# A decoder step's index stage: turns of keys and values one group later in buffers of their own, weight halves behind page requests, head sums in another bank

## The chip, the cores and the metric

The kernel runs on one core of a Trainium2 chip. The metric is the device time of one execution in microseconds. The core has TensorE (PE, matrix products), VectorE (DVE), ScalarE (ACT), GpSimd (POOL), SyncE (SP, which issues most transfers) and sixteen DMA engines.

## The reference

One layer of a hybrid decoder step: a prompt of 1024 tokens and eight decoding sequences of four new tokens each, with 8192 cached positions in pages of 128. An input projection feeds sparse attention (a lightweight indexer picks the 256 best keys) and retention; both are gated and merged. The change is in the part that scores the sequences' cached keys, beside which the prompt's queries, keys, values and gates are projected:

```python
def _project(h, w_in, pos):
    z = jnp.einsum('btd,de->bte', h, w_in)
    ...
    qa, ka, va, qi, ki, wi, ga, qb, kb, vb, gb = jnp.split(z, offsets, axis=-1)
    ...

def _index_select(qi, wi, ki, qpos, kpos, topk):
    s = jnp.einsum('bqhd,bsd->bqhs', qi.astype(jnp.float32), ki.astype(jnp.float32)) * (D_IDX ** -0.5)
    score = jnp.einsum('bqh,bqhs->bqs', wi.astype(jnp.float32), jax.nn.relu(s))
    ...
    top_val, top_idx = lax.top_k(score, topk)

def _dsa_sample(qa, ka, va, qi, ki, wi, cache_k, cache_v, cache_kidx, page_table, rel_bias):
    ...
    ki_past = cache_kidx[page_table].reshape(B, past, D_IDX).astype(ki.dtype)
    ki_all = jnp.concatenate([ki_past, ki], axis=1)
    idx, ok = _index_select(qi, wi, ki_all, qpos, kpos, topk)
    ...

def _merge(x, oa, ob, ga, gb, p, w_out, g_post, w_ple_up, w_ple_gate):
    ya = jax.nn.silu(ga) * oa.reshape(B, T, D_A).astype(x.dtype)
    ...
```

Outputs are the new hidden states, and the keys, values, index keys and retention states of this step.

## The kernel before

The kernel is one program in the Tile framework: the Python code names tiles and instructions, and a scheduler, which simulates a timeline, sets the order of each engine's instructions within what data, buffers and `issue_after` demand. So moving a line can move others. Buffers of one tag rotate: a new tile waits until the readers of the one it replaces are done.

Products are made in pairs of halves: each operand is split into a high part (`whi`, `xh`) and a rest (`wlo`, `xl`), and three products are summed. A projection of 128 columns (`proj_b`) runs over three groups of tokens (`GRP`) of 384, 416 and 256, in this order, with 8 x 3 = 24 matmuls for a group into a bank `pb`. `load_w` brings the weights of 256 columns in two halves `wraw`; for each half ACT makes `whi` by a cast (L202), and POOL subtracts four times for `wlo` (L203). Where `lazy` or `late` is given, `convert` is returned as a generator, and the steps are made by whoever draws on it.

The index stage (L854 to L938) loops over eight sequences `b` and two halves `a` of their pages. In each round POOL requests 1 MB of index keys by an indirect DMA (`key_pages`, L438) into one of two slabs `kx`; DVE transposes them (L913, twice); PE multiplies them with the queries into `pox` (L920); ACT takes the relu `rl` (L925). Then come:

- `later()`: the sum over heads of an earlier sequence (`head_sum`: PE into `py`, L881 and L884, then ACT's copy `ys`, L886), or its re-ordering by key (`by_key`: DVE `xv`, POOL `xe`).
- `step(bp)`: a pass of the bisection that finds the 256th score of the prompt's rows; ACT counts (`js`, L738), DVE counts (L740) and updates the bounds (`W`, `r`, L746 to L771). At its end a flag (`cf`, `pfl`) decides a branch (L805).
- `unit(...)`: one or two projection groups from `units()`: queries `qa`, then keys and values `kava`, then gates `ga0` and `ga1`.

For keys and values ACT copies the projection out of the bank into one half of `kvs` (L466). Ahead of the next group `triple` empties the list `turn`: PE transposes the copy (`kvt`, L475), ACT copies that into the other half of `kvs` (L477), and SP stores it. `kvs` has one buffer. Keys also get a split pair `kst` (ACT L488, DVE L489). For gates, ACT applies Silu to the bank into `sga` (L503), which SP stores. ACT loads the table that holds Silu once in the stage (ACT_TABLE_LOAD at L503).

PE's PSUM banks here: two of tag "b" (`pb`, and `py`), two of tag "t" (`kvt` and other turns), and two pairs of tag "S" (`pox`).

Of the kernel before, what the change touches and what calls it, by code (L numbers as in the profile page):

```python
# [11 lines left out]
F32 = mybir.dt.float32  # L12
# [4 lines left out]
AF = mybir.ActivationFunctionType  # L17
# [19 lines left out]
GRP = ((256, 384), (640, 416), (0, 256))  # L37
# [96 lines left out]
def tile_step(ctx: ExitStack, tc: tile.TileContext, I, O):  # L134
    nc = tc.nc
# [20 lines left out]
    cp = ctx.enter_context(pool("cp"))  # L156
# [3 lines left out]
    def bank(name, tag="b"):  # L160
        if tag in kept.get("tags", ()):
            return kept["pool"].tile([128, 512], F32, tag="s", bufs=1, name=name)
        of = psum["apart" if tag == psum["tag"] else "pool"]
        return of.tile([128, 512], F32, tag=tag, bufs=psum["bufs"][tag], name=name)

    def pair(name):
        return psum["pool"].tile([128, 1024], F32, tag="S", bufs=psum["bufs"]["S"], name=name)
# [3 lines left out]
    def C(name, rows=128):  # L171
        o, w = _CW[name]
        return cst[:rows, o:o + w]

    ident = C("ident")
# [46 lines left out]
    def wcols(*cols):  # L222
        return [(w_in[:, c:c + n], n) for c, n in cols]
# [208 lines left out]
    paged = [None]  # L432

    def key_pages(i):

        b, a = i // 2, i % 2
        kx = slab("kx").bitcast(F32).rearrange("p a b -> p (a b)")
        paged[0] = nc.gpsimd.indirect_dma_start(  # L438
            out=kx[:, :2048], out_offset=None, in_=pages,
            in_offset=bass.IndirectOffsetOnAxis(ap=kidx[:, a * 8 + b:a * 8 + b + 1], axis=0)).ins  # L440
        return kx
# [20 lines left out]

    def use_kv(g, pt, outs, outp, new, then=lambda tk: None):

        st = sx.tile([128, 2, 416], F32, tag="kvs", bufs=1, name="kvs")
        nc.scalar.copy(st[:, 0, :GRP[g][1]], pt[:, :GRP[g][1]])  # L466
        turn.append(lambda: then(turn_kv(g, st, outs, outp, new)))

    def turn_kv(g, st, outs, outp, new):

        t0, n = GRP[g]
        tp = bank("kvt", "t")
        for i in range(0, n, 128):
            rows = min(128, n - i)
            nc.tensor.transpose(tp[:rows, i:i + 128], st[:, 0, i:i + rows], ident)  # L475
        nb = NP[g]
        nc.scalar.copy(st[:, 1, :nb], tp[:, :nb])  # L477
        tk = st[:, 1, :nb].rearrange("p (b c) -> p b c", c=128)
        nc.sync.dma_start(outp[0, 0, t0:t0 + nb].rearrange("(b p) n d -> p b (n d)", p=128), tk)
        if g == SG:  # L480
            nc.vector.tensor_copy(new, tp[:NS, 384:512])
            nc.sync.dma_start(outs.rearrange("o b t n d -> (o b t) (n d)"), new)
        return tk
# [15 lines left out]

    def use_ga(j, g, pt):  # L500
        t0, n = GRP[g]
        sg = qsp.tile([128, 2, 416], F32, tag="qst", bufs=2, name="sga")
        nc.scalar.activation(sg[:, 0, :n], pt[:, :n], AF.Silu)  # L503
        nc.sync.dma_start(ga_d[:, j, t0:t0 + n], sg[:, 0, :n])

    def units():

        def triple(w, c0, use):
            for g in range(3):
                while turn:  # L510
                    turn.pop(0)()
                proj_b(w, c0, 128, use, (g,))
                yield

        w.extend([load_w("qa0", wcols((QA, 256))), load_w("qa1", wcols((QA + 256, 256)))])
        loads = [("kava", KA), ("ga0", GA), ("ga1", GA + 256), None]
        for i in range(5):
            for a in range(2):
                use = ((lambda g, pt: use_qa(2 * i + a, g, pt)) if i < 2 else
                       (use_ka, use_va)[a] if i == 2 else  # L520
                       (lambda g, pt: use_ga(2 * i - 6 + a, g, pt)))
                yield from triple(w[i], a * 128, use)
            if i < 3:
                w.append(load_w(loads[i][0], wcols((loads[i][1], 256)), late=0 if i else 3))

    w = []
    unit_gen = units()
    tick = [0.0]

# [322 lines left out]

    sp_one = cp.tile([128, 1], F32, name="sp_one")
    nc.gpsimd.memset(sp_one, 1.0)  # L854
    bp = bisect_prompt()

    def step(gen, n=1):
        for _ in range(n):
            next(gen, None)
# [5 lines left out]
    for up in range(2):  # L865
        nc.vector.tensor_tensor(wst[:, up], wcol[:, :, None].to_broadcast([128, 8, 32]),
                                C(f"wsel{up}")[:, None, :].to_broadcast([128, 8, 32]), op=ALU.mult)
    pn = bank("pn", "t")
    for h in range(8):
        nc.tensor.matmul(pn[:NS, h * 32:h * 32 + 32], qsn[:, h, :], kis, start=True, stop=True)  # L870
# [5 lines left out]
    nc.vector.tensor_tensor(newsc, newsc, C("nfill", 32), op=ALU.add)  # L876
    pend = []
    def head_sum(b, rls):
        py = bank("py")

        last_ = nc.tensor.matmul(py[96:128, :], wst[:, 1, b, :], rls[3], start=True, stop=True)  # L881
        with tc.issue_after(last_.ins):
            for i in range(3):
                nc.tensor.matmul(py[32 * i:32 * i + 32, :], wst[:, i % 2, b, :], rls[i], start=True, stop=True)  # L884
        ys = sx.tile([128, 512], F32, tag="ys", bufs=2, name="ys")
        nc.scalar.copy(ys, py)  # L886
        nc.sync.dma_start(xt_d[b], ys)
        pend.append(lambda: by_key(b, ys))
# [17 lines left out]
    for b in range(8):  # L906
        rls = []
        for a in range(2):
            kx = key_pages(2 * b + a) if b else kxs[a]
            po = pair("pox")  # L910
            kT = (kx[:, 2048:], kx[:, :1024])
            for up in range(2):
                nc.vector.transpose(kT[up], kx[:, up * 1024:up * 1024 + 1024])  # L913
            head = None
            for up in (1, 0):
                for u2 in range(2):
                    for r in range(2):
                        o, rr = 32 * (2 * (r ^ up) + u2), slice(r * 64, r * 64 + 64)
                        with (tc.issue_after(head) if head else ExitStack()):
                            mm = nc.tensor.matmul(po[o:o + 32, up * 512:up * 512 + 512], qbd[rr, b, :],  # L920
                                                  kT[up][rr, u2 * 512:u2 * 512 + 512], start=True, stop=True,
                                                  tile_position=(64 * r, o))
                        head = head or mm.ins
            rl = sx.tile([128, 1024], F32, tag="rl", bufs=3, name="rl")
            nc.scalar.activation(rl, po, AF.Relu)  # L925
            rls += [rl[:, :512], rl[:, 512:]]
            later()
            tickb[0] += 1.25
            while tickb[0] >= 1:
                tickb[0] -= 1  # L930
                step(bp)
            with tc.issue_after(scored[1]):
                unit((2, 2.5, 2, 2)[2 * b + a] if b < 2 else 12.5 / 12)
        pend.append(lambda b=b, rls=rls: head_sum(b, rls))
# [1167 lines left out]
```

## Time and profile before

| | |
|---|---|
| median of 3 runs | 974.04 us (972.46 to 976.85) |
| profiled execution | 971.68 us, span 969.9 us |
| mean clock granted to PE | 0.984 of full |
| PE busy | 917.9 us, 95% of the span |
| DVE, ACT, POOL busy | 639.4, 458.5, 318.8 us |

The profile is one execution's. A row of its timeline has an instruction's start, its duration, engine, line and tiles; brackets hold the idle time ahead of it and what ended that. A row of stretches gives each engine's busy time, then the clock granted to PE, the share of time that the DMA engines are busy, and GB/s. A row of the chain of waits says which engine and line waited for which, for how long in total, how often, and the longest. Matmuls overlap, so a group's time is read from the starts of its first and of the next group's first.

### The profile page before, as it was taken

How to read it: one execution, taken by the hardware profiler on the slowest of the kernel's cores; microseconds unless marked ns; L12 is line 12 of the kernel's file. 1: busy time of each engine (PE TensorE's matmuls, PEld its weight loads, DVE VectorE, ACT ScalarE, POOL GpSimd, SP SyncE). 2: the span in 40 equal slices, each digit the busy share in tenths (PEclk: the TensorE clock that was granted, in tenths of full speed). 3: DMA queues.
4: the chain of work that ended last, by engine and by line, in shares of the span. 5: the costliest groups of instructions: out<-in, count | busy, mean ns of one | idle time of the engine just before them, and what ended most of it. 6: DMA issues, size and time to landing. Idle time of an engine off the chain costs nothing.

```text
span 969.9 us, 19199 instructions
## 1 busy us (share of the span) xinstructions
PE 917.9 (95%) x7108; PEld 786.8 (81%) x7108; DVE 639.4 (66%) x1898; ACT 458.5 (47%) x1022; POOL 318.8 (33%) x442
## 2 busy tenths in 40 slices
PE   3999999888999999999999988999999999999998
PEld 2988788656779988899889965666668999999998
DVE  6837867878835669978888387877754234943332
ACT  5635654666323886425334284556555334422210
POOL 4205112312415414515344076545204422033300
PEclk8999999988999999999999999999999999999999
DMA  8413224676545110332145445433113222612211
GB/s 261 132 66 83 92 77 153 226 231 197 205 145 124 45 45 24 81 84 63 45 129 164 115 122 167 136 101 103 38 35 87 88 68 77 191 49 94 89 35 39
DMA packets 102129, 104.40 MB, mean 108 GB/s; under 512 B 22002, under 2 KB 92210, under 8 KB 99602
## 3 DMA queue, kind: packets, MB, share of 16 engines
q1 hardware_dynamic: 96274, 76.94, 26.8%
q0 software_dynamic: 5760, 26.22, 8.6%
q8 instruction: 56, 0.92, 0.4%
q14 instruction: 39, 0.32, 0.1%
HBM read 80.38 MB, written 22.76 MB: 106 GB/s over the span
## 4 chain that ended last, share of the span: by engine, by line
PE 54%; DVE 6%; issue 5%; DMA 3%; ACT 2%; POOL 1%; SPq 0%; DVEq 0%; ACTq 0%; POOLq 0%
PE pg L298 3%; PE pg L300 3%; PE pg L299 3%; PE ob L1866 3%; PE ptp L1858 3%; PE po L298 3%; PE po L300 3%; PE po L299 3%; PE pvg L299 2%; PE pvg L298 2%; PE pvg L300 2%; PE sa L1835 2%; PE pqk L298 2%; PE pqk L299 2%; PE pqk L300 2%
## 5 line engine op out<-in xcount | busy, mean ns | idle before, releaser
L1317 POOL DMA_INDIRECT kvs<-in_cache_kv,idx x64 | 67.5, 1054 | 81.8 <-PE pkg L1534 18.5
L298 PE MATMUL pvg<-whi_vgb,xh 128*128 128x256 f32 x256 | 75.2, 294 | 0.5 <-DVE rp L1153 0.5
L299 PE MATMUL pvg<-wlo_vgb,xh 128*128 128x256 f32 x256 | 73.5, 287 | 0.8 <-POOL wlo_vgb L203 0.8
L299 PE MATMUL pqk<-wlo_qkb,xh 128*128 128x256 f32 x256 | 73.9, 289 | 0.0
L298 PE MATMUL pqk<-whi_qkb,xh 128*128 128x256 f32 x256 | 73.8, 288 | 0.1
L300 PE MATMUL pvg<-whi_vgb,xl 128*128 128x256 f32 x256 | 73.7, 288 | 0.0
L300 PE MATMUL po<-whi_o,yTl 128*128 128x256 f32 x256 | 73.1, 285 | 0.4 <-POOL yTl L1914 0.4
L298 PE MATMUL po<-whi_o,yTh 128*128 128x256 f32 x256 | 73.2, 286 | 0.0
L299 PE MATMUL po<-wlo_o,yTh 128*128 128x256 f32 x256 | 72.9, 285 | 0.0
L298 PE MATMUL pg<-whi_g,yTh 128*128 128x256 f32 x256 | 72.8, 285 | 0.0
L300 PE MATMUL pqk<-whi_qkb,xl 128*128 128x256 f32 x256 | 72.8, 284 | 0.0
L300 PE MATMUL pg<-whi_g,yTl 128*128 128x256 f32 x256 | 72.4, 283 | 0.0
L299 PE MATMUL pg<-wlo_g,yTh 128*128 128x256 f32 x256 | 72.3, 283 | 0.0
L1845 ACT ACTIVATE L<-L,mn 128x128 f32<-128x128 f32 (+7 forms) x64 | 49.6, 776 | 22.5 <-DVE mn L1841 22.5
L2057 DVE TENSOR_TENSOR sgm<-pu,sgm 128x256 f32<-128x256 f32 x32 | 13.6, 424 | 64.4 <-PE pu L300 61.1
L203 POOL TENSOR_TENSOR wlo_g<-wraw_g,whi_g 128x256 fp32r<-128x256 f32 x32 | 27.2, 882 | 87.1 <-ACT whi_g L202 87.0
L1858 PEld LDWEIGHTS ptp<-cst,L 128*128 128x128 f32 x288 | 31.6, 142 | 23.8 <-issue 19.4
L298 PEld LDWEIGHTS po<-whi_o,yTh 128*128 128x128 f32 x256 | 49.1, 192 | 2.0 <-issue 1.6
L298 PEld LDWEIGHTS pvg<-whi_vgb,xh 128*128 128x128 f32 x256 | 48.4, 189 | 2.6 <-PE pvg L307 0.8
L298 PEld LDWEIGHTS pg<-whi_g,yTh 128*128 128x128 f32 x256 | 48.8, 191 | 1.6 <-issue 1.2
L569 DVE SCALAR_TENSOR_TENSOR score<-r,wi,score 128x384 f32<-128x384 f32 (+5 forms) x42 | 41.3, 984 | 13.1 <-ACT r L568 10.8
L300 PEld LDWEIGHTS po<-whi_o,yTl 128*128 128x128 f32 x256 | 49.1, 192 | 0.6 <-POOL yTl L1914 0.6
(536 smaller groups left out, 3058.7 us busy)
## 6 DMA issues: line engine op xcount, KB each, us to landing
wraw_qkb<-in_w_in SPq DMA_DIRECT2D x16, 256.0 KB
wraw_vgb<-in_w_in SPq DMA_DIRECT2D x16, 256.0 KB
qas<-qas_d SPq DMA_DIRECT2D x8, 512.0 KB
wraw_o<-in_w_out SPq DMA_DIRECT2D x8, 512.0 KB
xr<-in_x_prompt SPq DMA_DIRECT2D x8, 512.0 KB
wraw_g<-in_w_ple_gate SPq DMA_DIRECT2D x8, 512.0 KB
out_y_prompt<-sgm SPq DMA_DIRECT2D x32, 128.0 KB
qas_d<-qst SPq DMA_DIRECT2D x8, 384.0 KB
```

Source lines behind the costliest of these rows:

```text
L203: nc.gpsimd.tensor_tensor(lo[:, k, :n], raw, hi[:, k, :n].bitcast(F32), op=ALU.subtract)
L298: nc.tensor.matmul(pt[:, :n], ah, hi[:, k, :n], start=(k == 0), stop=False)
L299: nc.tensor.matmul(pt[:, :n], ah, lo[:, k, :n], start=False, stop=False)
L300: nc.tensor.matmul(pt[:, :n], al, hi[:, k, :n], start=False, stop=(k == kc - 1))
L569: nc.vector.scalar_tensor_tensor(sc, r[:, :n], wi[:, qb, h:h + 1], sc if h else place[:, :n], op0=ALU.mult, op1=ALU.add)
L1317: return nc.gpsimd.indirect_dma_start(out=dst, out_offset=None, in_=kvflat, in_offset=bass.IndirectOffsetOnAxis(ap=idx, axis=0))
L1835: nc.tensor.matmul(s[:, :wc], qas[:, h, :], kah[kv][:, c:c + wc], start=True, stop=False)
L1845: behind[0] = nc.scalar.activation(L[:, :n], L[:, :n], AF.Exp, bias=least, scale=-1.0, accum_out=sm[:, i4:i4 + 1])
L1858: nc.tensor.transpose(tp[:, i4 * 128:i4 * 128 + 128], P[i4][:, kb * 128:kb * 128 + 128], ident)
L1866: nc.tensor.matmul(ob[64 * o:64 * o + 64, :256], vtok[:, kb, kv * 64:kv * 64 + 64], pT[:, o * 256:o * 256 + 256], start=(kb == 0), stop=(k ...
L2057: nc.vector.tensor_tensor(sg[:rows], usrc, sg[:rows], op=ALU.mult)
```

## The change

- The copy out of the bank goes to `kva` (two buffers), the turned copy to `kvb` (one buffer), in place of the two halves of `kvs`. A turn is put on the list with a count of 2, which each group lowers; it is made at 0, so one group later than before.
- `sga` is a tile of half the size.
- The weights `ga0` and `ga1` are loaded lazily. Behind each page request (`issue_after(paged[0])`) two steps of the pending conversions are made; what is left is made ahead of the first group that uses the weights.
- `py` takes a bank of tag "t".
- An activation `sp_two` with Silu on a 1-wide tile is written ahead of the loop, where `sp_one` was made.

```diff
@@ -462,9 +462,9 @@
 
     def use_kv(g, pt, outs, outp, new, then=lambda tk: None):
 
-        st = sx.tile([128, 2, 416], F32, tag="kvs", bufs=1, name="kvs")
-        nc.scalar.copy(st[:, 0, :GRP[g][1]], pt[:, :GRP[g][1]])
-        turn.append(lambda: then(turn_kv(g, st, outs, outp, new)))
+        st = sx.tile([128, 416], F32, tag="kva", bufs=2, name="kva")
+        nc.scalar.copy(st[:, :GRP[g][1]], pt[:, :GRP[g][1]])
+        turn.append([2, lambda: then(turn_kv(g, st, outs, outp, new))])
 
     def turn_kv(g, st, outs, outp, new):
 
@@ -472,10 +472,11 @@
         tp = bank("kvt", "t")
         for i in range(0, n, 128):
             rows = min(128, n - i)
-            nc.tensor.transpose(tp[:rows, i:i + 128], st[:, 0, i:i + rows], ident)
+            nc.tensor.transpose(tp[:rows, i:i + 128], st[:, i:i + rows], ident)
         nb = NP[g]
-        nc.scalar.copy(st[:, 1, :nb], tp[:, :nb])
-        tk = st[:, 1, :nb].rearrange("p (b c) -> p b c", c=128)
+        kb = sx.tile([128, 384], F32, tag="kvb", bufs=1, name="kvb")
+        nc.scalar.copy(kb[:, :nb], tp[:, :nb])
+        tk = kb[:, :nb].rearrange("p (b c) -> p b c", c=128)
         nc.sync.dma_start(outp[0, 0, t0:t0 + nb].rearrange("(b p) n d -> p b (n d)", p=128), tk)
         if g == SG:
             nc.vector.tensor_copy(new, tp[:NS, 384:512])
@@ -499,31 +500,38 @@
 
     def use_ga(j, g, pt):
         t0, n = GRP[g]
-        sg = qsp.tile([128, 2, 416], F32, tag="qst", bufs=2, name="sga")
-        nc.scalar.activation(sg[:, 0, :n], pt[:, :n], AF.Silu)
-        nc.sync.dma_start(ga_d[:, j, t0:t0 + n], sg[:, 0, :n])
+        sg = qsp.tile([128, 416], F32, tag="qst", bufs=2, name="sga")
+        nc.scalar.activation(sg[:, :n], pt[:, :n], AF.Silu)
+        nc.sync.dma_start(ga_d[:, j, t0:t0 + n], sg[:, :n])
 
     def units():
 
         def triple(w, c0, use):
             for g in range(3):
-                while turn:
-                    turn.pop(0)()
+                for t in turn:
+                    t[0] -= 1
+                while turn and not turn[0][0]:
+                    turn.pop(0)[1]()
                 proj_b(w, c0, 128, use, (g,))
                 yield
 
         w.extend([load_w("qa0", wcols((QA, 256))), load_w("qa1", wcols((QA + 256, 256)))])
         loads = [("kava", KA), ("ga0", GA), ("ga1", GA + 256), None]
         for i in range(5):
+            if i > 2:
+                for _ in w[i][3]:
+                    pass
             for a in range(2):
                 use = ((lambda g, pt: use_qa(2 * i + a, g, pt)) if i < 2 else
                        (use_ka, use_va)[a] if i == 2 else
                        (lambda g, pt: use_ga(2 * i - 6 + a, g, pt)))
                 yield from triple(w[i], a * 128, use)
             if i < 3:
-                w.append(load_w(loads[i][0], wcols((loads[i][1], 256)), late=0 if i else 3))
-
-    w = []
+                w.append(load_w(loads[i][0], wcols((loads[i][1], 256)), lazy=i > 0, late=0 if i else 3))
+                if i:
+                    halves.append(w[-1][3])
+
+    w, halves = [], []
     unit_gen = units()
     tick = [0.0]
 
@@ -852,6 +860,7 @@
 
     sp_one = cp.tile([128, 1], F32, name="sp_one")
     nc.gpsimd.memset(sp_one, 1.0)
+    sp_two = cp.tile([128, 1], F32, name="sp_two")
     bp = bisect_prompt()
 
     def step(gen, n=1):
@@ -865,6 +874,7 @@
     for up in range(2):
         nc.vector.tensor_tensor(wst[:, up], wcol[:, :, None].to_broadcast([128, 8, 32]),
                                 C(f"wsel{up}")[:, None, :].to_broadcast([128, 8, 32]), op=ALU.mult)
+    nc.scalar.activation(sp_two, sp_one, AF.Silu)
     pn = bank("pn", "t")
     for h in range(8):
         nc.tensor.matmul(pn[:NS, h * 32:h * 32 + 32], qsn[:, h, :], kis, start=True, stop=True)
@@ -876,7 +886,7 @@
     nc.vector.tensor_tensor(newsc, newsc, C("nfill", 32), op=ALU.add)
     pend = []
     def head_sum(b, rls):
-        py = bank("py")
+        py = bank("py", "t")
 
         last_ = nc.tensor.matmul(py[96:128, :], wst[:, 1, b, :], rls[3], start=True, stop=True)
         with tc.issue_after(last_.ins):
@@ -907,6 +917,9 @@
         rls = []
         for a in range(2):
             kx = key_pages(2 * b + a) if b else kxs[a]
+            with tc.issue_after(paged[0]):
+                for half in halves:
+                    step(half, 2)
             po = pair("pox")
             kT = (kx[:, 2048:], kx[:, :1024])
             for up in range(2):
```

The order of the instructions, at three places. PE, where the first keys' group of 384 tokens is done (about 180 us): what comes ahead of the group of 416 tokens (`pb` with `whi_kava`). Before:

```order
L920 MATMUL pox<-kx,qbd 32x512
L920 MATMUL pox<-kx,qbd 32x512 [waits DMASW3_49,DVE_49,Activation_49]
L920 MATMUL pox<-kx,qbd 32x512 x7
L881 MATMUL py<-rl,wst 32x512 [waits DVE_49,PE_49]
L884 MATMUL py<-rl,wst 32x512 x3
L475 MATMUL kvt<-cst,kvs 128x128 [waits Activation_49]
L475 MATMUL kvt<-cst,kvs 128x128 x2
L288 MATMUL pb<-xh,whi_kava 128x416
```

and with the change:

```order
L933 MATMUL pox<-kx,qbd 32x512
L891 MATMUL py<-rl,wst 32x512 [waits Activation_49]
L894 MATMUL py<-rl,wst 32x512 x3
L933 MATMUL pox<-kx,qbd 32x512 [waits DMASW3_49,DVE_49,PE_49]
L933 MATMUL pox<-kx,qbd 32x512 x7
L288 MATMUL pb<-xh,whi_kava 128x416 [waits DVE_49,PE_49]
...
L475 MATMUL kvt<-cst,kva 128x128 [waits Activation_49]
L475 MATMUL kvt<-cst,kva 128x128 x2
L288 MATMUL pb<-xh,whi_kava 128x256
```

The turn `kvt` stood ahead of the group of 416 and waits for ACT's copy; now it stands behind that group's 24 matmuls and ahead of the group of 256.

POOL, from the requests of this time on (`kx` is a page request; `wlo_ga` are the subtractions for `ga0`, then `ga1`). Before:

```order
L438 DMA kx<-in_cache_kidx,kidx 128x2048 x2
L203 TENSOR_TENSOR wlo_ga_1767<-wraw_ga_1768,whi_ga_1766 128x256 x4
L203 TENSOR_TENSOR wlo_ga_1767<-wraw_ga_1770,whi_ga_1766 128x256 x4
L438 DMA kx<-in_cache_kidx,kidx 128x2048 x2
L894 COPY xe<-xv 128x16x8x2
L438 DMA kx<-in_cache_kidx,kidx 128x2048 x3
L894 COPY xe<-xv 128x16x8x2
L438 DMA kx<-in_cache_kidx,kidx 128x2048
L203 TENSOR_TENSOR wlo_ga_2196<-wraw_ga_2197,whi_ga_2195 128x256 x4
L203 TENSOR_TENSOR wlo_ga_2196<-wraw_ga_2199,whi_ga_2195 128x256 x4
```

and with the change:

```order
L438 DMA kx<-in_cache_kidx,kidx 128x2048 x2
L203 TENSOR_TENSOR wlo_ga_1769<-wraw_ga_1770,whi_ga_1768 128x256 x4
L438 DMA kx<-in_cache_kidx,kidx 128x2048
L203 TENSOR_TENSOR wlo_ga_1769<-wraw_ga_1772,whi_ga_1768 128x256 x2
L438 DMA kx<-in_cache_kidx,kidx 128x2048
L203 TENSOR_TENSOR wlo_ga_1769<-wraw_ga_1772,whi_ga_1768 128x256 x2
L904 COPY xe<-xv 128x16x8x2
L438 DMA kx<-in_cache_kidx,kidx 128x2048 x2
L904 COPY xe<-xv 128x16x8x2
L203 TENSOR_TENSOR wlo_ga_2192<-wraw_ga_2193,whi_ga_2191 128x256 x4
L438 DMA kx<-in_cache_kidx,kidx 128x2048
L203 TENSOR_TENSOR wlo_ga_2192<-wraw_ga_2195,whi_ga_2191 128x256 x2
```

The subtractions of both weight pairs now alternate with page requests and `xe`; `ga1`'s first four stand ahead of a request that they stood behind.

ACT, at the start of the program. Before:

```order
L608 ACT_TABLE_LOAD
L608 ACTIVATE warm<-warm 128x1
L597 ACTIVATE score,ss<-x_123 128x1024
L270 ACTIVATE ry_x_161<-rv_x_159 128x1
L597 ACTIVATE score,ss<-x_124 128x1024
```

and with the change:

```order
L616 ACT_TABLE_LOAD
L616 ACTIVATE warm<-warm 128x1
L877 ACT_TABLE_LOAD
L877 ACTIVATE sp_two<-sp_one 128x1
L605 ACTIVATE score,ss<-x_123 128x1024
L270 ACT_TABLE_LOAD
L270 ACTIVATE ry_x_161<-rv_x_159 128x1
L605 ACTIVATE score,ss<-x_124 128x1024
```

The scheduler has moved `sp_two` and its table load to the start, where the root (`ry_x`, L270) needs a table load again; the load at the first `sga` is still there (L504 in the new numbering). PE's branch on the flag also moves: between `pfl` and the branch stood ten matmuls of a page's product and a group of 256 tokens, and now a head sum and 13 matmuls of a group. Behind the stage, PE's order is the same until the attention part, where the scheduler has ordered the same instructions differently on PE, ACT and DVE, in the stretch that ran at about 560 to 770 us.

## The prediction

> **What bounds the kernel now.** I read the first page for the bound, then the engines by stretches of time, then TensorE's (PE's) own timeline for its gaps, then the chain of waits inside those gaps. The page first: busy time by engine.
>
> ```profile
> span 969.9 us, 19199 instructions
> PE 917.9 (95%) x7108; PEld 786.8 (81%) x7108; DVE 639.4 (66%) x1898; ACT 458.5 (47%) x1022; POOL 318.8 (33%) x442
> ```
>
> PE is busy for 95% of the span, so a change helps only by closing the 52 us in which it is idle, or by raising the clock it runs at. Stretches (PE, weight load, DVE, ACT and POOL busy, then the granted clock) show where these lie; the changed loop runs from about 150 to 291 us.
>
> ```profile
> 150.00:180.00 30.00, 27.87 (x194) 23.89 (x192) 24.60 (x53) 13.44 (x22) 9.53 (x10) 1.00 0.56 185
> 180.00:240.00 60.00, 49.46 (x331) 36.84 (x330) 48.63 (x128) 38.25 (x68) 17.32 (x24) 0.89 0.73 233
> 240.00:291.00 51.00, 50.74 (x380) 38.62 (x382) 32.47 (x47) 16.18 (x25) 13.29 (x20) 1.00 0.48 167
> 560.00:770.00 210.00, 201.52 (x1579) 142.05 (x1578) 139.53 (x502) 120.48 (x276) 95.25 (x97) 0.99 0.35 101
> ```
>
> Between 180 and 240 us PE is idle for 60 - 49.46 = 10.54 us, and at a clock of 0.89 it loses up to 0.11 x 60 = 6.6 us more. From 240 us on there is nothing to win. PE's timeline names each gap (start of the instruction that ended it; in brackets its length and releaser).
>
> ```profile
> 185.61 0.55 PE L475 MATMUL kvt<-cst,kvs 128*128 128x128 f32 x3 [2.37 <-ACT kvs L466]
> ...
> 194.74 1.09 PE L920 MATMUL pox<-kx,qbd 64*32 64x512 f32 x16 [1.19 <-DVE r L770]
> 197.12 0.76 PE L475 MATMUL kvt<-cst,kvs 128*128 128x128 f32 x4 [1.28 <-ACT kvs L466]
> ...
> 214.13 1.58 PE L920 MATMUL pox<-kx,qbd 64*32 64x512 f32 x16 [2.18 <-DVE kx L913]
> ...
> 228.99 1.06 PE L881 MATMUL py<-rl,wst 128*32 128x512 f32 x1 [3.52 <-ACT sga L503]
> ```
>
> The five add to 2.37 + 1.19 + 1.28 + 2.18 + 3.52 = 10.54 us, all of the idle time. Four-microsecond stretches behind the gaps give the clock:
>
> ```profile
> 183.00:187.00 4.00, 1.63 (x13) 1.39 (x10) 3.73 (x11) 1.92 (x4) 2.69 (x4) 1.00 0.85 229
> 197.00:201.00 4.00, 3.88 (x15) 3.87 (x16) 3.00 (x9) 3.97 (x8) 0.15 (x1) 0.57 0.95 289
> 214.00:218.00 4.00, 3.87 (x27) 2.57 (x28) 3.73 (x16) 2.70 (x5) 1.32 (x2) 0.58 1.01 346
> 231.00:235.00 4.00, 4.00 (x13) 3.84 (x14) 3.28 (x14) 3.80 (x7) 0.42 (x1) 0.50 0.95 321
> ```
>
> So gaps cost twice: the pair 1.19 + 1.28, the 2.18 and the 3.52 were each followed by about half clock, the 2.37 was not. One drop lost 4 x 0.43 = 1.7 us, the last one longer. What the stage waits for, in the chain of waits of 150 to 300 us (total, times, longest):
>
> ```profile
> POOL wlo_ga L203 <- ACT whi_ga L202: 9.5, 2, 6.7
> ...
> ACT kvs L466 <- DMA out_k_prompt<-kvs: 3.7, 2, 2.5
> ...
> ACT kvs L466 <- DVE kst L489: 2.8, 1, 2.8
> ```
>
> **The change, part by part.**
>
> *Turns one group later, `kva` in two buffers, `kvb` apart.* In PE's order before, the turn `kvt` stands ahead of the next projection group and has to wait for ACT's copy of the last one; that copy waits for `kst` (2.8) or for the output DMA that still reads the one `kvs` buffer (3.7 in two waits). Now a whole group stands between. The 2.37 gap goes. The 1.28 one shrinks to about 0.25, by laying out ACT's new order: the copy has two buffers, but is still queued behind relu and bisection passes. What is late next is the turned copy in its single `kvb` buffer, waiting for its output DMA on ACT, with `rl` queued behind. Six such copies have five successors; the nearest price is 0 to 2.5 each (longest above). I take 0, since their groups are 3 to 5 us apart, and keep 12.5 for the range. The half-size `sga` tile changes no instruction's shape, and SP's queue only sends one store of `ys` ahead of a weight half that nobody waits for there: 0.
>
> *Weight halves two at a time behind the page requests.* No instruction is added: 8 subtractions per weight pair, the same 2 casts. Before, all 8 of `ga0` stand ahead of two page requests on POOL; now 4, a request, 2, a request, 2. Then come page landing, two DVE transposes, and PE. The requests cannot leave before PE frees the slab, so this moves a page by at most the four subtractions. `wlo_ga1` moves the other way: four of its subtractions now stand ahead of a request that had none ahead. The page stalls 1.19 and 2.18 should both go where the order is early, but DVE sets a new one. Its rows and the durations for laying out PE's new order:
>
> ```profile
> 224.33 1.23 DVE L913 STREAM_TRANSPOSE kx<-kx 128x1024 f32<-128x1024 f32 x1
> 225.50 0.30 DVE L771 TENSOR_TENSOR W<-W,r 128x6 f32<-128x6 f32 x1
> 225.72 1.23 DVE L913 STREAM_TRANSPOSE kx<-kx 128x1024 f32<-128x1024 f32 x1
> ```
>
> ```profile
> 244.56 0.44 PE L288 MATMUL pb<-xh,whi_ga 128*128 128x384 f32 x1
> ...
> 248.88 0.36 PE L288 MATMUL pb<-xh,whi_ga 128*128 128x416 f32 x1
> ...
> 253.47 0.62 PE L881 MATMUL py<-rl,wst 128*32 128x512 f32 x1
> ...
> 254.47 1.09 PE L920 MATMUL pox<-kx,qbd 64*32 64x512 f32 x16
> 255.49 0.39 PE L288 MATMUL pb<-xh,whi_ga 128*128 128x256 f32 x1
> ...
> 258.44 0.34 PE L288 MATMUL pb<-xh,whi_ga 128*128 128x384 f32 x1
> ```
>
> At full clock a group of 384 takes 248.88 - 244.56 = 4.32 us, of 416 4.59, of 256 2.95, a head sum 1.00, a page's product 1.02. With these I laid PE's new order out from 180 us, holding DVE's chain of bisection passes at its old times, since it does not depend on PE. PE reaches `pox_2370` at about 225.0; its transposes end at 225.72 + 1.23 = 226.95: a stall of 1.95. Further on, two products wait about 0.65 and 0.45 for their transposes (walked in the same way).
>
> *Head sums in the turns' banks.* `py` used the projection's two banks and so waited for `sga`, the copy out of one of them; ACT was in a bisection pass and then in a table load:
>
> ```profile
> 225.89 1.15 ACT L738 ACTIVATE js<-score,W 128x1024 bf16<-128x1024 f32 x1 [3.79 <-DVE W L771]
> 226.94 0.19 ACT L738 ACTIVATION_READ_ACCUMULATOR js<-score,W 128x1 f32 x1
> 227.15 1.28 ACT L503 ACT_TABLE_LOAD   x1
> 228.44 0.49 ACT L503 ACTIVATE sga<-pb 128x384 f32<-128x384 f32 x1
> ```
>
> With `py` beside `kvt` that gap of 3.52 goes, whether the load is there or not: the nearest things it can now wait for are ACT's copies of `ys` and `kvb`, of about the 0.49 of the last row, and they lie beside other groups: 0.
>
> *Gate table first.* It does not do what it says. The order has `sp_two` at the start of the program, and the load at L504 stands in the stage as before. The new cost is two loads of 1.28 us (row above) and 0.2, near this place:
>
> ```profile
> 4.49 1.06 ACT L597 ACTIVATE score<-x 128x1024 bf16<-128x1024 f32 x1 [2.25 <-DMA x<-in_x_prompt]
> ...
> 5.85 0.20 ACT L270 ACTIVATE ry_x<-rv_x 128x1 f32<-128x1 f32 x1 [0.22 <-DVE rv_x L267]
> ```
>
> ```profile
> 8.60 1.28 DVE L599 SCALAR_TENSOR_TENSOR x<-x,ry_x,mask 128x1024 f32<-128x1024 f32 x1 [1.32 <-DMA mask<-in_g_pre]
> ```
>
> The first load and `sp_two`, 1.5 us, lie in the 2.25 us that ACT waits for x. The second delays the root at 5.85 by about 1.1; behind it DVE waits 1.32 for a DMA in any case. Bounds 0 and 1.3; I take 0.1. If that DMA came earlier, the 1.1 would show. The Trainium skill, "ScalarE: Activation LUTs", "What ACT_TABLE_LOAD costs", speaks against this part: it adds a drain of about 1.38 us to each load, 2.66 in all, and by that the start would cost some 1.5 us more. The rows at 227.15 and 228.44 leave no room for a drain ahead of the next activation, so the sum is without it.
>
> *The flag.* PE's branch on the bisection's flag moves. Rows of PE and DVE:
>
> ```profile
> 269.94 0.15 DVE L791 TENSOR_REDUCE cf<-cf 128x1 f32<-128x6 f32 x1
> ```
>
> ```profile
> 270.50 0.19 PE L703 MATMUL pfl<-sp_one,cf 128*1 128x1 f32 x2
> ...
> 274.99 1.09 PE L920 MATMUL pox<-kx,qbd 64*32 64x512 f32 x16 [0.26 <-DVEq L805]
> ```
>
> Laid out, DVE delivers `cf` at about 260.5 and PE stands ready 2.15 earlier; DVE is 81% busy from 180 to 240 us, so it cannot be pulled along as far as PE. From `pfl` to the branch took 274.99 - 270.50 = 4.5 us; the new order has 1.00 + 13/24 x 4.32 = 3.3 us of work in between (a head sum, 13 matmuls): 1.2, against 0.26.
>
> *Elsewhere.* The order also shuffles attention instructions on PE, ACT and DVE in about 560 to 770 us, with no new work. PE is idle there for 210 - 201.52 = 8.48 us. Bounds: all of that gone, or as much again; I take 0.
>
> **The sum.** Removed: 10.5 us of gaps and about 6.0 of the 6.6 lost to the clock, together 16.5. New: 0.25 + 1.95 + 0.65 + 0.45 + 2.15 + 1.2 - 0.26 = 6.4. One drop of the clock behind the two stalls of about 2 us, since of gaps of that size one was followed by a drop and one was not: 1.5. The start: 0.1. Net 16.5 - 8.0 = 8.5 us. Everything behind the stage is bound by PE (96% in 560:770), so it carries through. The profiled execution took 971.68 us, 2.4 under the median of 974.04: 971.68 - 8.5 = 963.2 in its terms, 965.5 against the median.
>
> The Trainium skill, "TensorE: Matmul & The Clock Gate", "HAM oscillation", gives as the rule that only idle gaps over some 3.4 us cost the clock, and Part 1 of that page that the windows run freely. By the rule alone no new stall would lower it, and the sum would be 1.5 us better, 964.0; the gap of 2.18 that was followed by 0.58 speaks against it, the free windows fit both.
>
> **Rivals.** *Pages become the bound.* PE runs ahead, the two slabs and a busy DVE do not: the new stalls double to 12.8 and two clock drops come, 3.0, so 16.5 - 15.8 = 0.7 us are saved: about 973.3. For it: DVE 81% busy (48.63 of 60); against: page waits now sum to 3.4 us only. The `kvb` wait ends here too. Chance 0.21.
>
> *A late half holds the page requests (slower).* Two requests now stand behind subtractions that wait for ACT's cast of a later half. That wait was up to 6.7 us. Twice 6.7 and one more drop, 1.5, are 14.9: 16.5 - 8.0 - 14.9 = -6.4, so 980.4. It decides from 8.5 us of delay; the loss shows in a measurement from 13.4. Against it: ACT's casts stand early enough in the new order, and the requests wait for PE anyway. The reshuffled attention could do the same only with its full 8.48 and more. Chance 0.08.
>
> *No stall remains*, bisection passes being pulled ahead by ACT: 16.5 us, 957.5. Against it is DVE's load. Chance 0.11, my forecast 0.60.
>
> **Numbers.** Half a per cent (4.9 us) is about what a measurement here tells from no change: faster is below 969.2, slower above 978.9. Forecast and best case together, less 0.01 of the forecast's tail, give faster 0.70; the page bound and that tail 0.22; slower 0.08. The range runs from the best case to the page bound, 957.5 to 973.5; the forecast's own is 960.5 to 969.
>
> **What would show it.** Right: no gap at L475 over 0.5, none at the head sum; gaps at `pox` near 225 and at the flag near 260; loop end near 282; two more table loads at the start, one still in the stage. Wrong: PE idle more than 9 us in the stage, a clock under 0.95 over it, ACT waiting on `out_k_prompt<-kvb`, or PE idle in 560 to 770 us changed by over 3.

## The result and the profile after

The changed kernel takes 962.44 us (median of 6 runs, 960.44 to 965.05) against 973.6 before (6 runs): a ratio of 0.9889, 95% interval 0.9861 to 0.9917, so 8 to 14 us less. Forecast were 965.5 and 8.5 us. The profiled execution took 962.92 us, 8.8 less than the one before.

First the stretches (PE, weight load, DVE, ACT, POOL busy, then the granted clock):

```profile
180.00:240.00 60.00, 56.02 (x420) 44.58 (x420) 54.42 (x135) 39.19 (x70) 17.35 (x23) 1.00 0.79 262
240.00:281.00 41.00, 38.86 (x310) 29.88 (x310) 25.00 (x41) 11.98 (x18) 12.06 (x24) 1.00 0.53 177
```

From 180 to 240 us PE is idle for 4.0 us instead of 10.54, and the clock is full where it was 0.89. A little of the idle time has moved behind 240 us: 2.1 there. PE's timeline, all gaps over 0.2 us in the stage:

```profile
189.17 1.09 PE L933 MATMUL pox<-kx,qbd 64*32 64x512 f32 x16 [1.40 <-issue]
...
223.63 0.66 PE L933 MATMUL pox<-kx,qbd 64*32 64x512 f32 x8 [2.40 <-issue]
...
250.95 1.09 PE L933 MATMUL pox<-kx,qbd 64*32 64x512 f32 x16 [0.79 <-issue]
...
255.65 0.17 PE L711 MATMUL pfl<-sp_one,cf 128*1 128x1 f32 x1 [1.36 <-DVE cf L799]
```

No gap over 0.2 us stands at a turn (L475) or a head sum (L891) any more. Those left are at the page products and the flag. At the page products "issue" says that the profile shows no releaser, but DVE's rows do: its second transpose of the page ends 0.1 us before each of the three products. For the longest gap this is the row, which ends at 223.54:

```profile
222.29 1.25 DVE L926 STREAM_TRANSPOSE kx<-kx 128x1024 f32<-128x1024 f32 x1
```

To compare kernels I use one length, the *stage*: from the first `kava` product to the first `pqk` product with `whi`. Before and after, these rows of PE's timeline bound it:

```profile
175.76 0.42 PE L288 MATMUL pb<-xh,whi_kava 128*128 128x384 f32 x1
...
291.89 0.39 PE L298 MATMUL pqk<-whi_qkb,xh 128*128 128x256 f32 x1
```

```profile
172.40 0.42 PE L288 MATMUL pb<-xh,whi_kava 128*128 128x384 f32 x1
...
276.68 0.38 PE L298 MATMUL pqk<-whi_qkb,xh 128*128 128x256 f32 x1
```

116.13 before, 104.28 after: 11.9 us less. The first row is 3.4 us earlier in the changed kernel, though PE's order up to there is the same; in the kernels below it lies between 172.4 and 176.9, so I count that as a difference between executions. The granted clock fits this: over the first 100 us it was 0.93 before and 0.97 here. Another length goes the other way, the *attention* interval, from the third `dst` product to the first `pty` product. Before, then after:

```profile
445.49 0.58 PE L1299 MATMUL dst<-vm,kvst 128*128 128x512 f32 x1
...
734.87 0.60 PE L1918 MATMUL pty<-cst,yb 128*128 128x128 f32 x4
```

```profile
430.99 0.58 PE L1312 MATMUL dst<-vm,kvst 128*128 128x512 f32 x1
...
725.04 0.60 PE L1931 MATMUL pty<-cst,yb 128*128 128x128 f32 x4
```

289.4 before, 294.1 after: 4.7 us given back in this execution. Only 1.6 of these are idle time (PE is idle for 9.7 us of the interval before and 11.3 after); PE's busy time is 3.1 longer, at a granted clock of 0.98 instead of 0.99. So the 8.8 us of the profiled executions are made up of 3.4 us less ahead of the stage, 11.9 less in it, 0.7 more between it and the attention interval, 4.7 more in that, and 1.0 more behind it.

### The profile page after: what moved, and what is told of

Same layout as the page of the kernel before. It is cut to its first block, busy times and chain, and to the rows that moved or that the text cites. A ratio compares the mean times of both kernels' runs of the same rounds, so it can differ in the third digit from the quotient of the medians.

```text
span 961.1 us, 19195 instructions
## 1 busy us (share of the span) xinstructions
PE 911.5 (95%) x7108; PEld 780.9 (81%) x7108; DVE 641.6 (67%) x1898; ACT 460.6 (48%) x1025; POOL 315.5 (33%) x442
## 4 chain that ended last, share of the span: by engine, by line
PE 66%; DVE 13%; issue 6%; DMA 6%; ACT 3%; SPq 3%; POOL 1%; another core or an unknown queue 0%; DVEq 0%; ACTq 0%; POOLq 0%
PE pb L288 4%; PE pb L290 4%; PE pb L289 4%; PE pg L298 3%; PE pg L300 3%; PE pg L299 3%; PE ob L1879 3%; PE ptp L1871 3%; PE po L298 2%; PE pvg L299 2%; PE pvg L298 2%; PE pvg L300 2%; PE po L300 2%; PE po L299 2%; PE sa L1848 2%
## 5 line engine op out<-in xcount | busy, mean ns | idle before, releaser
L1330 POOL DMA_INDIRECT kvs<-in_cache_kv,idx x64 | 65.5, 1023 | 94.8 <-ACT L L1858 22.8
L2069 ACT ACTIVATE sgm<-pg 128x256 f32<-128x256 f32 x32 | 12.3, 385 | 79.3 <-PE pg L300 74.6
L298 PEld LDWEIGHTS pqk<-whi_qkb,xh 128*128 128x128 f32 x256 | 48.2, 188 | 2.5 <-issue 0.6
```

Of the source, the lines that this page charges most:

```text
L298: nc.tensor.matmul(pt[:, :n], ah, hi[:, k, :n], start=(k == 0), stop=False)
L1330: return nc.gpsimd.indirect_dma_start(out=dst, out_offset=None, in_=kvflat, in_offset=bass.IndirectOffsetOnAxis(ap=idx, axis=0))
```

## The experiments

All twelve in one table; each ratio is to the kernel before on the same chip, with its 95% interval. Stage and attention are worked out as above, from two rows of each kernel's own timeline; "order" says whether the attention part's instructions stand as before (B), as in the changed kernel (C), or otherwise. Each stage and each attention interval is that of one execution; the two of the changed kernel differ by 0.7 and 1.5 us, and of the kernel before there is one.

| kernel | what it has | ratio | stage | attention, order |
|---|---|---|---|---|
| before | | 1 | 116.1 | 289.4 B |
| changed | all | 0.9889 (0.9861 to 0.9917) | 104.3 | 294.1 C |
| again | all, once more | 0.9918 (0.9893 to 0.9944) | 105.0 | 292.6 C |
| u_gate | all but early Silu | 0.9911 (0.9878 to 0.9945) | 103.3 | 291.9 C |
| kva1 | all, one `kva` buffer | 0.9918 (0.9884 to 0.9952) | 104.9 | 291.0 C |
| u_halves | all but lazy halves | 0.9897 (0.9859 to 0.9934) | 105.2 | 290.5 other |
| u_delay | all but later turns | 0.9926 (0.9901 to 0.9951) | 105.3 | 291.3 other |
| u_bank | all but the bank | 1.0038 (1.0014 to 1.0061) | 115.1 | 292.8 other |
| u_turns | all but turns and buffers | 1.0113 (1.0072 to 1.0153) | 123.7 | 289.9 B |
| b_bank | the bank alone | 1.0074 (1.0045 to 1.0103) | 118.0 | 290.9 other |
| b_turns | turns and buffers alone | 1.0027 (1.0003 to 1.0051) | 112.1 | 292.6 other |
| b_halves | lazy halves alone | 1.0062 (1.0034 to 1.0090) | 115.4 | 294.1 other |
| m_two | bank, buffers apart | 0.9945 (0.9923 to 0.9966) | 108.9 | 291.0 B |
| m_two_gate | m_two, table load earlier | 0.9927 (0.9908 to 0.9947) | 109.3 | 289.8 B |

**One part undone (first four).** The first expectations give the attention interval by two other rows (a later `dst` product and a later `pty` product, picked because both had idle time ahead). I replaced them by the two rows above, which all kernels have.

u_bank:

```diff
-        py = bank("py", "t")
+        py = bank("py")
```

> The change with one part undone: the head sums' py takes a bank of tag b again. My theory: py shares its bank with a projection group, so it waits for ACT's Silu copy behind a bisection pass and the table load once more; a gap of 2 to 3.5 us at the head sum and a drop of the clock behind it come back, 3 to 6 us over the changed kernel (962.4), so 965.5 to 968.5. Rival: the turns' later place has moved the head sums away from the Silu copies, and the time stays within 1 us of the changed kernel. Part of the difference can come from another order of the attention part (the kernels' orders differ there): PE's time from the L1312 product to the first L1931 product, 317.1 us in the changed kernel and 312.5 before, is to be taken off first.

It was worse than expected: 975.43 us, slower than the kernel before. PE's gaps:

```profile
184.48 0.46 PE L288 MATMUL pb<-xh,whi_kava 128*128 128x416 f32 x1 [2.00 <-ACT kva L466]
...
218.38 1.09 PE L933 MATMUL pox<-kx,qbd 64*32 64x512 f32 x16 [1.70 <-issue]
...
220.98 0.71 PE L288 MATMUL pb<-xh,whi_ga 128*128 128x416 f32 x1 [1.51 <-ACT sga L504]
...
258.69 1.09 PE L933 MATMUL pox<-kx,qbd 64*32 64x512 f32 x16 [2.35 <-issue]
...
271.64 1.11 PE L933 MATMUL pox<-kx,qbd 64*32 64x512 f32 x8 [2.95 <-issue]
```

The wait is not at the head sum but at the projection groups: `py` sits in one of their two banks, and the next group waits for ACT's copy out of the other. Two page gaps of 2.35 and 2.95 come late in the stage. The five add to 10.5 us, where the changed kernel's four had 6.0. The other 6 us of the longer stage are PE's busy time, 104.2 us against 98.2, with the clock at 0.57 from 220 to 228 us and again from 271 to 275.

u_halves takes `lazy`, the two steps behind each request and the drain ahead of `ga0` out again:

```diff
-            with tc.issue_after(paged[0]):
-                for half in halves:
-                    step(half, 2)
```

> The change with one part undone: ga0 and ga1 are converted at once, eight subtractions in a row ahead of the page requests, as before. My theory: the requests wait mostly for PE to free a slab, so this part is worth little: 0 to 2 us over the changed kernel's index stage, a page stall of at most 2 us more. Rival (the late half would have slowed the change): the stage gets faster without it, by 1 us or more. Second rival: the split of the halves carries the removal of the stalls at the page products (1.19 and 2.18 before, each with a clock drop), and the stage is 4 us or more slower.

962.24 us, stage 105.2: no loss that shows. The first theory holds, and both rivals fall.

u_turns goes back to one `kvs` buffer and turns ahead of the next group; the diff is that part of the change, reversed.

```diff
-        st = sx.tile([128, 416], F32, tag="kva", bufs=2, name="kva")
+        st = sx.tile([128, 2, 416], F32, tag="kvs", bufs=1, name="kvs")
...
-        turn.append([2, lambda: then(turn_kv(g, st, outs, outp, new))])
+        turn.append(lambda: then(turn_kv(g, st, outs, outp, new)))
```

> The change with one part undone: one kvs buffer again, turns ahead of the next group. My theory: the gaps of 2.37 and 1.28 at L475 come back and part of a clock drop, 4 to 7 us in the index stage. Its attention part has the instruction order of the kernel before; if the order is what cost the changed kernel 4.6 us there, PE's time from the L1312 product to the first L1931 product is 312.5 as before, and the whole is only 0 to 2 us over the changed kernel. Rival: the 4.6 us were an accident of one execution, that interval is anywhere between 312 and 317, and the whole is 4 to 7 us slower than the changed kernel.

982.73 us, slower than the kernel before, and a stage 19 us over the changed kernel's where 4 to 7 were expected. Its largest gaps:

```profile
198.91 1.96 PE L930 MATMUL pox<-kx,qbd 64*32 64x512 f32 x16 [4.00 <-ACT js L743]
...
214.84 0.55 PE L475 MATMUL kvt<-cst,kvs 128*128 128x128 f32 x3 [1.71 <-ACT kvs L466]
...
233.43 0.71 PE L288 MATMUL pb<-xh,whi_ga 128*128 128x416 f32 x1 [5.82 <-ACT sga L503]
...
269.53 0.19 PE L708 MATMUL pfl<-sp_one,cf 128*1 128x1 f32 x2 [4.45 <-DVE cf L796]
```

Three of the four wait for ACT. ACT is held up itself, once by the store that still reads `kvs`, as this row of its timeline shows:

```profile
207.73 0.37 ACT L466 COPY kvs<-pb 128x256 f32<-128x256 f32 x1 [1.51 <-DMA out_k_prompt<-kvs]
```

u_gate leaves `sp_two` out.

```diff
-    nc.scalar.activation(sp_two, sp_one, AF.Silu)
```

> The change without the early Silu (sp_two): two table loads and one activation fewer at the start, all else in the same order. My theory: both loads are covered at the start by transfers that DVE and ACT wait for, so the time is within 0.5 us of the changed kernel, and the load at the first gate stays where it is. Rival: the load of 1.28 us (or 2.66 with a drain) on the path of the first root delays all by 1 to 1.5 us, and the time falls by as much. The attention part has the changed kernel's order: its interval should be 317 again if the order sets it.

961.99 us: the early Silu neither costs nor gives anything that can be measured.

**One part alone, and the turns taken apart.** b_bank has only `bank("py", "t")`, b_turns only the turns, their buffers and the small `sga`.

> The kernel before with one part of the change alone: py in tag t. My theory, formed after u_turns (stage from the first kava product to the first pqk product with whi 123.7 us, against 116.1 before): the bank alone does not pay, because py then queues for the two t banks with turns whose copies ACT makes late; stage 116 to 122, time 972 to 978. Rival: the bank alone takes away the 3.5 us gap at the head sum and the half clock behind it, stage 110 to 112, time 967 to 969; then it is the halves that hurt in u_turns.

> The kernel before with the turns alone (kva in two buffers, kvb apart, one group later, small sga tile); py stays in tag b, weights converted at once. My theory, after u_bank (stage 115.1): py between the projections takes one of their two banks and a group has to wait for ACT's copy of the one before, so the stage is 113 to 116 and the time 970 to 974. Rival: it is the lazy halves that cost the 11 us in u_bank, and turns alone give a stage of 106 to 109, time 963 to 966.

975.58 and 971.1 us: as expected, neither pays in time, and both are slower than the kernel before, b_turns by little. But its stage of 112.1 is 4.0 us shorter than before and below the 113 that I had given: no gap is left at L475. In their place projection groups wait 1.27, 2.11 and 0.56 us for ACT's copies out of their bank, and the attention interval is 3.2 longer. In b_bank PE has lost the gap at the head sum and got this one (first row), behind ACT rows that explain it:

```profile
229.11 0.69 PE L475 MATMUL kvt<-cst,kvs 128*128 128x128 f32 x2 [4.68 <-ACT kvs L466]
```

```profile
225.14 1.15 ACT L738 ACTIVATE js<-score,W 128x1024 bf16<-128x1024 f32 x1 [4.33 <-DVE W L771]
...
226.41 1.04 ACT L738 ACTIVATE js<-score,W 128x896 bf16<-128x896 f32 x1
...
227.58 0.94 ACT L738 ACTIVATE js<-score,W 128x768 bf16<-128x768 f32 x1
228.42 0.19 ACT L738 ACTIVATION_READ_ACCUMULATOR js<-score,W 128x1 f32 x1
228.68 0.37 ACT L466 COPY kvs<-pb 128x256 f32<-128x256 f32 x1
```

Before, the head sum waited 3.52 us for the gate's copy, queued behind a bisection count and the table load on ACT; with the bank moved, the turn, which stood behind the head sum and now stands ahead of it, waits 4.68 for the keys' and values' copy, queued behind three counts of one pass. The bank alone turns one wait into another. ACT itself had stood idle ahead of the first of these counts for 4.33 us, until DVE had updated the bounds (`W`); so at this place the late engine behind ACT's queue is DVE with its bisection.

The kernels with one part undone keep the halves, and that matters: u_turns has 5.7 us more stage than b_bank, and u_bank 3.0 more than b_turns. The first two differ in the halves, the early Silu and the small `sga`, the others in the halves and the early Silu. So what u_turns and u_bank lose is not all the price of the part left out. Which of these lengthens the stage there wasn't tried; taken out of the whole change, neither the halves nor the early Silu shows.

u_delay keeps buffers, bank and halves, and makes each turn ahead of the next group; kva1 keeps the later turns with one `kva` buffer.

```diff
-        turn.append([2, lambda: then(turn_kv(g, st, outs, outp, new))])
+        turn.append(lambda: then(turn_kv(g, st, outs, outp, new)))
```

```diff
-        st = sx.tile([128, 416], F32, tag="kva", bufs=2, name="kva")
+        st = sx.tile([128, 416], F32, tag="kva", bufs=1, name="kva")
```

> The change with separate buffers, bank and halves as they are, but each turn made ahead of the next group, as before. Tells the later place from the buffers. My theory: the later place is what counts, since PE stands still at the turn while ACT copies; gaps at L475 of 1 to 2.5 us come back and the stage is 110 to 118, time 968 to 976. Rival: the single buffer's wait for its store was the larger part, and the stage is within 2 us of the changed kernel's 104.3.

> The change with kva in one buffer instead of two, turns one group later as in the change. My theory: with the turn behind the next group the copy of that next group must wait for the turn, which is done by then; stage 104 to 106, time 962 to 964. Rival: a copy held back by the one buffer holds the projection's bank, and the stage is 107 us or more. The attention part has the changed kernel's order: PE's time from the first dst product to the first pty product should be 292 to 294 as there (291.9 and 294.1), not 289.5 as in the two kernels with the order of before.

961.72 and 960.45 us. My theory of the later place falls: at L475 one gap of 0.51 comes back, and the stage is within 1 us of the changed kernel's. kva1 came out as expected in its stage; its time is below the 962 to 964 given, its attention interval of 291.0 below the 292 to 294.

**The two parts together, and the rest.** m_two has the bank and the copies apart, and nothing more:

```diff
-        st = sx.tile([128, 2, 416], F32, tag="kvs", bufs=1, name="kvs")
+        st = sx.tile([128, 416], F32, tag="kva", bufs=1, name="kva")
...
+        kb = sx.tile([128, 384], F32, tag="kvb", bufs=1, name="kvb")
...
-        py = bank("py")
+        py = bank("py", "t")
```

> The kernel before with two parts alone: the copy out of the bank in kva (one buffer) and the turned copy in kvb, turns ahead of the next group as before; and py in tag t. No later turns, no lazy halves, no early Silu, sga as before. My theory: these two parts together are the whole gain in the index stage, each of them alone being none: stage 104 to 106 us (116.1 before, 104.3 changed), ratio 0.985 to 0.992. The order of its attention part is that of the kernel before; if order costs anything there, its interval is 289 to 290.5 and it beats the changed kernel by 2 to 3 us. Rival: the later turns or the halves stand in for one another in u_halves and u_delay, and without both the stage is 109 us or more. Second rival: the attention interval is 290 to 294 whatever the order.

965.51 us. The bank alone is at 1.0074, the turns with more than these copies apart (b_turns) at 1.0027, and bank and copies together at 0.9945, with 7.2 us off the stage where the bank alone had lengthened it by 1.9. So they act together; the copies apart by themselves, with turns in place, weren't tried. But "the whole gain" was too much: 4 to 5 us of the stage are missing, and the first rival comes within 0.1 us of the 109 it gave. The kernel doesn't beat the changed one either, and its attention interval of 291.0 is above the range. The largest gap in the stage says where:

```profile
192.91 0.66 PE L475 MATMUL kvt<-cst,kva 128*128 128x128 f32 x4 [2.50 <-ACT kva L466]
```

With turns in place, one buffer and the halves at once, this turn still waits, and behind it the clock was 0.57 from 193 to 197 us, another 1.7 us (4 x 0.43). u_delay (a second buffer, halves), u_halves (a second buffer, later turns) and kva1 (later turns, halves) each leave one of the three out and lose about 1 us of stage at most. Which pair is needed wasn't tried. All three also have the small `sga`, which m_two lacks; no run takes that alone, so it isn't excluded.

m_two_gate adds a Silu that reads `wst`, so that its load can't go to the start:

```diff
+    nc.scalar.activation(sp_two, wst[:, 0, 0, :1], AF.Silu)
```

> m_two and a one-wide Silu that reads wst, so that it can't be moved to the start: the order shows the table load behind the first sequence's relu, some 45 rows ahead of its place at the first gate, and no load more. My theory: ACT waits for other engines at both places and py no longer waits for the gate's copy, so the time is within 1 us of m_two. Rival: the load of 1.28 us in the stage still holds up the copies that free the banks, and the stage is 1 to 2 us shorter than that of m_two.

963.4 us against 965.51, with intervals that overlap, and a stage of 109.3 against 108.9: an earlier load shortens nothing in the stage.

> The changed kernel itself once more, for its profile and a comparison on one chip with m_two. Ratio 0.987 to 0.992. Its attention interval was 294.1, and 291.9 in u_gate and 291.0 in kva1, which have the same order there: if the order sets it, 291 to 294 again; if it is an accident of the execution, it may be as low as 289.

The ratio is as expected, the attention interval 292.6.

> The kernel before with the weight halves alone. My theory: nothing gained, as undoing them cost nothing: stage 114 to 118, ratio 0.997 to 1.004. Rival: the requests come earlier and the stalls at the page products (1.19 and 2.18 with a clock drop each) go, so the stage is 110 to 112.

975.49 us, stage 115.4: no gain in the stage, as expected, but the whole is slower than the 1.004 that I had given as the upper end. Its attention interval of 294.1 is 4.7 us longer than that of the one execution before.

**The attention order.** With the order of the kernel before the interval was 289.4, 289.9, 291.0 and 289.8, with that of the changed kernel 294.1, 292.6, 291.9 and 291.0. The means differ by 2.4 us, the values of one order by up to 3.1. So the changed order probably costs some 2 us; from eight executions that is not shown.

## Why the prediction was right

The time, its sign and the kind of mechanism were right; the account by parts was not.

- *The sum.* New stalls were put at 6.4 us; the profile has 1.40 + 0.17 + 2.40 + 0.79 + 1.36 = 6.1 (the 0.17 at a turn). The 1.95 at the product near 225 came as 2.40 at 223.63, and for the reason given, DVE's transposes; the 0.65 and 0.45 as one of 0.79, the flag's 2.15 as 1.36; the 1.2 at the branch did not come. The 1.19 at the early page product was struck out and is still there, as 1.40.
- *The clock* was the term of the sum that was mis-sized. 6.0 us back less 1.5 for a new drop made 4.5; in the stage 11.9 us went, 4.7 of them idle time (10.54 + 0.26 to 6.1), and the remaining 7.2 fit PE running at full clock (0.89 of 60 us before gave up to 6.6). A new drop did occur in another execution: the changed kernel run again has it behind a gap of 2.98, where the first had 2.40. Rows of the run again:

```profile
226.57 1.09 PE L933 MATMUL pox<-kx,qbd 64*32 64x512 f32 x16 [2.98 <-issue]
```

```profile
225.00:235.00 10.00, 8.43 (x51) 5.95 (x52) 9.69 (x24) 5.28 (x10) 0.95 (x1) 0.83 0.91 310
```

  So the one expected drop is a matter of the execution, with 1.7 us (10 x 0.17) where it comes. By the rule of the Trainium skill, "TensorE: Matmul & The Clock Gate", "HAM oscillation", no gap of the changed kernel is long enough to cost the clock; the trace has a drop behind this one of 2.98, as the one before has behind 2.18, so it does not hold in this kernel.
- *Attention* was put at 0 with bounds of 8.48 either way; it was +4.7 in the first profile, +3.2 in the second against 289.4. So the closeness of the profile's 8.8 to the 8.5 is in part luck: the stage alone gave 11.9, the stretches behind it took 6.4 back, and 3.4 came from ahead of the stage, where PE's order is the same.
- *Part by part* is where the working failed. The sum gave the 2.37 and 1.28 to the turns, the 3.52 to the bank and the 2.18 to the halves, as if each could be had alone. b_bank, b_turns and b_halves alone each gain nothing in time, and of their stages only that of b_turns is shorter by more than 1 us (4.0). The head sum's, the turns' and the projections' waits all have ACT's queue behind them, as the releasers in the rows above show, and PE takes its instructions in the program's order: when the wait ahead is taken away, PE stands at the next instruction that needs the same queue. The step "that gap of 3.52 goes" was true of the place and not of the time.
- *Halves* were to remove the 1.19 and the 2.18. u_halves has gaps of 0.29, 0.78 and 0.62 at its page products without them, so they weren't the cause. The 1.19 was also misread as a late page. Before, DVE made the transpose that this product needed without idle time ahead of it, between other work (first row, ending at 194.68); only the 2.18 stood behind a page that landed late (second row):

```profile
193.45 1.23 DVE L913 STREAM_TRANSPOSE kx<-kx 128x1024 f32<-128x1024 f32 x1
...
211.51 1.25 DVE L913 STREAM_TRANSPOSE kx<-kx 128x1024 f32<-128x1024 f32 x1 [3.24 <-DMA kx<-in_cache_kidx,kidx]
```

- *Later turns* were said to close the turn's gaps; u_delay has only 0.51 there without them.
- *Gate table first* was right: the load stays in the stage (a row of ACT's timeline), and the two at the start don't show.

```profile
212.03 1.28 ACT L504 ACT_TABLE_LOAD   x1
```

- *The rivals.* Pages holding up PE is half there: all stalls over 0.2 us but the flag's are at `pox`, 4.6 us there where 3.05 were laid out, yet with the flag's they made 6.1 and not 12.8. The late half did not delay requests in a way that shows: undoing it left stage and time as they were. That no stall remains is false by these 6.1 us.
- *The signs.* Those named for being right came; the loop ended earlier than given (276.7 for 282). One named for being wrong came too: PE's idle time from 560 to 770 us went from 8.48 to 4.54. But some 10 us of that window hold other instructions now, since all runs earlier; between the two rows of the attention interval the idle time changed by 1.6.

## What to carry to other kernels

When several waits on an in-order engine have one late engine behind them, price them together: taking one away moves the stall to the next, and a part tried alone can look harmful though the whole pays. Two changes that free banks and buffers of the same chain should be timed as a pair before either is thrown out. Where a scheduler sets the order, look also at stretches that the edit doesn't touch, and compare a fixed interval between two instructions rather than whole spans: here the stage showed 11 to 12 us where the whole showed 7 to 11.

## What the runs showed of the hardware

Two table loads more at the start cost nothing that the times show (ratios of 0.9889 and 0.9918 with them, 0.9911 without). With them the first root comes later, at 6.84 us in the changed kernel where it came at 5.85 before:

```profile
5.54 1.28 ACT L270 ACT_TABLE_LOAD   x1
6.84 0.20 ACT L270 ACTIVATE ry_x<-rv_x 128x1 f32<-128x1 f32 x1
```

The activation starts 0.02 us behind the load's end. Idle gaps of 2.37 (before) and 2.40 (after) left PE's clock at 1.00, gaps of 2.18 (before, 0.58 in the four microseconds that follow) and 2.98 (the run again, 0.83 from 225 to 235 us) did not. In u_delay the clock was 0.57 from 192 to 196 us behind gaps of 1.38 and 0.51. So the length of one gap of this size does not decide it.
